# Grouping the diagonal blocks for the stream transposes, and writing out TensorE's order from the latents to the recurrence, in a two-layer RWKV-7/MLA decoder kernel

## The chip, the cores and the metric

The kernel runs on one core of a Trainium2 chip. TensorE multiplies matrices and writes PSUM; VectorE, ScalarE and GpSimd (POOL in the rows) work on SBUF and, but for GpSimd, on PSUM; SyncE (SP) issues nearly all DMAs. Every engine works through its own queue in order and waits on semaphores for the others. The metric is the device time of one execution in microseconds, the median of several runs. All data is float32.

## The reference

Two layers, each a mixer and a gated feed-forward, at 512 tokens and width 1024. The mixer projects once, runs an RWKV-7 time mix of 8 heads x 64 and a latent attention of 8 heads, and adds both under gates. What matters here is the state of the time mix and what is around it:

```
p = n @ w_in                                  # r, k, v, loras, MLA latents, gates
def step(state, inp):                         # 512 tokens, 8 heads, state 64x64
    sa = einsum('bhij,bhj->bhi', state, a_t)
    state = state * w_t + sa[..., None] * b_t + v_t[..., None] * k_t
    y_t = einsum('bhij,bhj->bhi', state, r_t)
y_a = group_norm(y) + bonus, gated, @ w_out_rwkv
q = rmsnorm(q_lat) @ w_q_up; kv = rmsnorm(kv_lat) @ w_kv_up; causal softmax attention
merged = sigmoid(g_A) * y_a + sigmoid(g_B) * y_b
h = h + merged @ w_out; h = h + conv_ffn(rmsnorm(h))
```

The kernel doesn't run the 512 steps one by one: it cuts them into 8 chunks of 64 tokens. Within a chunk the terms between tokens form a lower triangular 64x64 matrix for each head and chunk, and its inverse is needed; from chunk to chunk a state of 64x64 for each head is carried.

## The kernel before

Activations lie transposed, features on partitions and the 512 tokens along the free axis. All weights come as one stream of 512 KB units; `produce` loads one (SP), `parts` splits it in a rounded part on ScalarE (`whi`, L201) and a rest on VectorE (`wlo`, L202), and `Blocks` hands out 128x128 blocks. A product of a block is three matmuls (`mm3`, L246 to L248), a tile of 8 blocks (`wtile`) is 24 matmuls into one PSUM tile `acc`.

`mixer` runs in three pools. In `ta` (up to L596) the inputs of the time mix are made; at its end VectorE writes the masked chunk matrices `AM` (L569). In `ti` (L614 to L738) the following is done; names and lines are those of the profile:

- four latent tiles `lat` (L623 to L626, evicted by VectorE), their squares on ScalarE (L629), one addition of two squares on GpSimd (L630), column sums on TensorE (`tok_sums`, L305), a reciprocal root (`rsqrt_tok`: VectorE L285, GpSimd L286, ScalarE `nw` L288) and a spread by TensorE transposes (L294).
- L643: for each pair of chunks the products of AM and v, copied into `Z` by ScalarE (L647).
- the inverse of the triangular matrices. Each 64x64 matrix has two diagonal blocks of 32x32, so AM holds four groups of partitions ("quad") with 32 matrices each. VectorE transposes the four groups, one instruction each (L665), into `X`, then does a forward substitution of 30 steps on all of X at once (L669, L671), and transposes back: four times into AM (L674) and twice into `T11` (L676). The lower left block follows with TensorE: AM x T11 (L685), copied to `Q` by VectorE and ScalarE (L688), Q x the second diagonal block (L692), copied to AM (L696). This comes in two halves of 16 matrices (`b`).
- the recurrence over the 8 chunks c: state x AR (L709), `xs` on VectorE (L712), AM x xs (L718), copy to Z (L720), BT x Z (L726), and the new state `St` on VectorE (L733) from a product on GpSimd (L732). Each of the steps waits for the one before it.
- four gate tiles (`gate`), each a `wtile`, an eviction on VectorE (L436), a tanh on ScalarE (L450) and a store to `gate_d`.

In `tb` (from L740) come the value product `Vt` (L826), chunk outputs (L756, L764), group norm, and four attention head pairs (`heads`), with the projections, scores (L852), softmax, transposes (L863) and `po` (L870).

The order in each engine's queue isn't that of the source: Tile's scheduler sets it, so gate tiles and the attention of the first head pairs come to stand between the pieces of the inverse and of the recurrence, where it saw room. Weights keep their order in the stream: latents, the gate tiles, the up-projections.

Of the kernel before, what the change touches and what calls it, by code (L numbers as in the profile page):

```python
# [9 lines left out]
F32 = mybir.dt.float32  # L10
F32R = mybir.dt.float32r
I32 = mybir.dt.int32
AF = mybir.ActivationFunctionType
# [145 lines left out]
def build(ctx, tc, x, pos, wst, vecd, constd, out):  # L159
# [95 lines left out]

    def acc():
        return accp[-1].tile([128, 512], F32, name="acc", tag="acc")
# [23 lines left out]
    def rsqrt_tok(ps, n, eps, js=range(4), pool=sm, tag="nsq"):  # L281
# [5 lines left out]
        w = pool.tile([128, 512], F32, name="nw", tag=tag, bufs=1)  # L287
# [15 lines left out]
    def tok_sums(ps, sq, js=range(4)):  # L303
        for j in js:
            PE.matmul(ps[:, j:j + 1], sq[:, 128 * j:128 * j + 128], ones[:, 0:1], start=True, stop=True)  # L305
# [93 lines left out]
    def mixer(l, ops, nrm, wks):  # L399
        with ExitStack() as mx:  # L400
# [213 lines left out]
            with pool(name=f"ti{l}", bufs=2) as ti:  # L614
# [6 lines left out]
                lat = []  # L621
                for i in range(4):
                    ps = wtile(ops)  # L623
# [3 lines left out]
                sq = [ti.tile([128, 512], F32, name="lsq", bufs=3) for _ in range(3)]  # L627
                for i in range(3):
                    A.activation(sq[i], lat[i], AF.Square)  # L629
                G.tensor_tensor(sq[0], sq[0], sq[1], ALU.add)  # L630
                ws = []
                for i, (t, n) in enumerate(((sq[0], 256.0), (sq[2], 128.0))):
                    ssq = sc()
                    tok_sums(ssq, t)
                    ws.append(rsqrt_tok(ssq, n, NORM_EPS, pool=ti, tag=f"nw{i}"))


                for i in range(4):
# [10 lines left out]
                rq = tl.tile([128, 512], F32, name="rq", bufs=1)  # L649
                spread(ws[0], tabs[1], rq, sc)  # L650
                rk = ti.tile([128, 512], F32, name="rk", bufs=1)
                spread(ws[1], None, rk, sc)
                V.scalar_tensor_tensor(lat[2], lat[2], vc(l, "kv_norm"), rk, ALU.mult, ALU.mult)
                kp = tl.tile([128, 512], F32, name="kp", bufs=1)
                k2 = ti.tile([128, 512], F32, name="k2", bufs=1)
# [5 lines left out]
                X = ti.tile([128, 32, 32], F32, name="X", bufs=1)  # L661
                T11 = ti.tile([128, 32, 32], F32, name="T11", bufs=1)
                quad = [((0 if e else 64) + 32 * hf, (128 if e else 64) + 32 * hf, hf) for e in range(2) for hf in range(2)]
                for r0, c0, hf in quad:
                    V.transpose(X[r0:r0 + 32], AMu[r0:r0 + 32, :, c0:c0 + 32].rearrange("p u t -> p t u"))  # L665
                for s in range(1, 31):
                    tm = ti.tile([128, 256], F32, name="tm", tag="tm", bufs=2)
                    tm = tm[:, 0:(31 - s) * s].rearrange("p (a b) -> p a b", b=s)
                    V.tensor_tensor(tm, X[:, s + 1:32, s:s + 1].to_broadcast([128, 31 - s, s]),  # L669
                                    X[:, s:s + 1, 0:s].to_broadcast([128, 31 - s, s]), ALU.mult)  # L670
                    V.tensor_tensor(X[:, s + 1:32, 0:s], X[:, s + 1:32, 0:s], tm, ALU.add)  # L671
                V.memset(X.rearrange("p a b -> p (a b)")[:, 0:1024:33], 1.0)
                for r0, c0, hf in quad:
                    V.transpose(AMu[r0:r0 + 32, :, c0:c0 + 32].rearrange("p u t -> p t u"), X[r0:r0 + 32])  # L674
                    if hf == 0:
                        V.transpose(T11[r0:r0 + 32].rearrange("p u s -> p s u"), X[r0:r0 + 32].rearrange("p t s -> p s t"))  # L676
                gate(GATES[4][0], ti)
                half = [(64, 64), (0, 128)]
                for b in range(2):
                    us = range(16 * b, 16 * b + 16)  # L680
                    Q = ti.tile([128, 512], F32, name="Q", bufs=2).rearrange("p (u s) -> p u s", s=32)
                    ps = xyt()[:, b, :]
                    for u in us:
                        for r0, c0 in half:
                            PE.matmul(ps[r0 + 32:r0 + 64, 32 * (u % 16):32 * (u % 16) + 32], AMu[r0:r0 + 32, u, c0 + 32:c0 + 64],  # L685
                                      T11[r0:r0 + 32, u, :], start=True, stop=True, tile_position=(r0, r0 + 32))
                    for r0, c0 in half:
                        (A.copy if r0 else V.tensor_copy)(Q[r0 + 32:r0 + 64], ps[r0 + 32:r0 + 64, :].rearrange("p (u s) -> p u s", s=32))  # L688
                    ps = xyt()[:, b, :]
                    for u in us:  # L690
# [46 lines left out]
                for i in GATES[4][1:]:  # L737
                    gate(i, ti)  # L738
# [252 lines left out]
```

## Time and profile before

| what | value |
|---|---|
| median of 3 runs | 1616.56 us (1616.34 to 1618.22) |
| profiled execution | 1616.36 us |
| its span in the trace | 1614.6 us |
| TensorE busy | 97% of the span |
| VectorE, ScalarE, GpSimd busy | 58%, 40%, 12% |

Stages of the first layer in that trace: the last AM is there at 184.9 us, the latents begin at 183.0, the first matmul of the inverse at 234.7, the recurrence runs from 256.4 to 301.3. The second layer goes through the same some 796 us later. A busy matmul row is a modelled one, so "busy" says that the engine didn't wait, not that it ran at its peak; the granted clock is read beside it.

### The profile page before, as it was taken

Reading aid. Unit: us, or ns where it says so; the run is one execution under the profiler, and the core shown is the slowest. Engines: PE = TensorE matmul, PEld = TensorE weight load, DVE = VectorE, ACT = ScalarE, POOL = GpSimd, SP = SyncE. Lnnn points to the kernel's source line nnn. Section 1 sums busy time; section 2 is a strip of 40 time slices with the busy share of each in tenths; the row PEclk is TensorE's granted clock in tenths of the full one; section 3 lists DMA queues with packets and bytes.
Section 4 is the critical chain, followed back from the end, with each engine's and each line's share of the span. In section 5 each row is a group of like instructions: output and inputs, shape, how many; then the busy total and the mean of one; then the engine's idle time right before and its main releaser. Section 6 shows DMA issues by size and latency. Waiting matters only on the chain.

```text
span 1614.6 us, 22337 instructions
## 1 busy us (share of the span) xinstructions
PE 1568.8 (97%) x9014; PEld 1259.1 (78%) x9014; DVE 942.0 (58%) x1482; ACT 651.0 (40%) x987; POOL 190.4 (12%) x158
## 2 busy tenths in 40 slices
PE   8999989999999999999999999899999999999997
PEld 6888766668888888888877887666788888888886
DVE  6578786666545555533347668857564555554333
ACT  6446334563434333422245342346533433333221
POOL 1011101300211101100011111023003111110000
PEclk9999999999999999999999999899999999999998
DMA  6333312224322323233343233212243223232232
GB/s 212 107 111 119 114 57 86 67 73 156 124 90 94 104 92 102 94 108 121 111 150 98 98 98 111 73 47 82 92 156 116 90 93 104 92 101 95 95 101 79
DMA packets 57848, 166.08 MB, mean 103 GB/s; under 512 B 6416, under 2 KB 9616, under 8 KB 57744
## 3 DMA queue, kind: packets, MB, share of 16 engines
q1 hardware_dynamic: 57600, 164.48, 31.1%
q8 instruction: 71, 1.16, 0.3%
q14 instruction: 33, 0.27, 0.1%
q10 hardware_dynamic: 144, 0.16, 0.0%
HBM read 147.32 MB, written 17.30 MB: 102 GB/s over the span
## 4 chain that ended last, share of the span: by engine, by line
PE 79%; issue 10%; DVE 7%; POOL 2%; ACT 1%; DMA 0%; POOLq 0%; DVEq 0%; SPq 0%; ACTq 0%
PE acc L246 22%; PE acc L248 22%; PE acc L247 22%; PE sc L852 2%; PE po L870 2%; PE xy L718 1%; PE pt L863 1%; DVE AM L674 1%; DVE X L665 1%; DVE wlo L202 1%; POOL mu L781 1%; PE m L566 1%; DVE tm L669 1%; DVE X L671 1%; POOL nv L286 1%
## 5 line engine op out<-in xcount | busy, mean ns | idle before, releaser
L246 PE MATMUL acc<-hi,whi 128*128 128x512 f32 (+1 forms) x1910 | 751.4, 393 | 8.4 <-ACT hi L267 5.3
L248 PE MATMUL acc<-hi,wlo 128*128 128x512 f32 (+1 forms) x1910 | 747.1, 391 | 0.7 <-DVE wlo L202 0.7
L247 PE MATMUL acc<-lo,whi 128*128 128x512 f32 (+1 forms) x1910 | 745.7, 390 | 0.0
L201 ACT CAST whi<-raw 128x1024 fp32r<-128x1024 f32 (+2 forms) x249 | 253.3, 1019 | 541.0 <-PE acc L247 479.3
L246 PEld LDWEIGHTS acc<-hi,whi 128*128 128x128 f32 x1910 | 360.9, 189 | 83.6 <-ACT hi L267 5.3
L248 PEld LDWEIGHTS acc<-hi,wlo 128*128 128x128 f32 x1910 | 361.2, 189 | 77.4 <-issue 2.1
L247 PEld LDWEIGHTS acc<-lo,whi 128*128 128x128 f32 x1910 | 361.2, 189 | 73.4 <-issue 1.2
L202 DVE TENSOR_TENSOR wlo<-raw,whi 128x1024 fp32r<-128x1024 f32 (+2 forms) x249 | 308.3, 1239 | 182.0 <-ACT whi L201 181.2
L942 POOL TENSOR_TENSOR c<-c,rstd 128x512 f32<-128x512 f32 x44 | 57.3, 1304 | 377.9 <-ACT c L941 377.9
L935 DVE TENSOR_TENSOR u<-acc,rstd 128x512 f32<-128x512 f32 x44 | 30.3, 691 | 100.2 <-PE acc L248 94.4
L944 DVE TENSOR_TENSOR c<-c,acc 128x512 f32<-128x512 f32 x44 | 30.2, 687 | 82.4 <-POOL c L942 82.4
L941 ACT ACTIVATE c<-c 128x512 f32<-128x512 f32 x44 | 27.6, 632 | 78.7 <-DVE c L940 78.7
L286 POOL TENSOR_TENSOR nv<-nv,cst 128x4 f32<-128x4 f32 (+1 forms) x10 | 12.8, 1288 | 332.8 <-DVE nv L285 332.8
L321 POOL TENSOR_TENSOR nacc<-nacc,nsq 128x512 f32<-128x512 f32 x14 | 25.0, 1788 | 201.7 <-ACT nsq L320 201.7
L858 ACT ACTIVATE P<-P,mn 128x128 f32<-128x128 f32 (+3 forms) x64 | 35.5, 556 | 26.1 <-DVE mn L855 22.8
L852 PE MATMUL sc<-K,q 128*128 128x128 f32 (+3 forms) x128 | 44.5, 447 | 0.0
L424 DVE TENSOR_TENSOR cur<-acc,rstd 128x512 f32<-128x512 f32 x28 | 19.1, 690 | 43.0 <-PE acc L248 38.5
L436 DVE TENSOR_TENSOR gg<-acc,rstd 128x512 f32<-128x512 f32 x28 | 19.2, 686 | 36.9 <-PE acc L248 36.7
L860 ACT ACTIVATE P<-P,mn 128x128 f32<-128x128 f32 (+3 forms) x64 | 34.8, 558 | 8.8 <-DVE mn L859 8.8
L870 PE MATMUL po<-PT,Vt 128*64 128x128 f32 x320 | 37.5, 286 | 0.8 <-DVE PT L865 0.8
L938 ACT ACTIVATE c<-u,vec 128x512 f32<-128x512 f32 x44 | 35.4, 809 | 2.3 <-DVE u L935 1.5
L855 DVE CUSTOM_DVE_ANT_0 P<-sc,cst 128x128 f32<-128x128 f32 (+3 forms) x64 | 30.6, 480 | 9.2 <-PE sc L852 5.3
(233 smaller groups left out, 1393.8 us busy)
## 6 DMA issues: line engine op xcount, KB each, us to landing
raw<-in_w SPq DMA_DIRECT2D x238, 512.0 KB, 3.4
gate_d<-gg SPq DMA_DIRECT2D x32, 256.0 KB, 2.1
AM<-gate_d SPq DMA_DIRECT2D x16, 256.0 KB, 4.6
gb<-gate_d SPq DMA_DIRECT2D x16, 256.0 KB, 3.7
h<-in_x SPq DMA_DIRECT2D x8, 256.0 KB, 4.3
rgate_d<-gt SPq DMA_DIRECT2D x8, 256.0 KB, 3.0
bl_d<-rk SPq DMA_DIRECT2D x8, 256.0 KB, 2.0
bl<-bl_d SPq DMA_DIRECT2D x8, 256.0 KB, 2.6
```

What stands on the lines that cost most here:

```text
L201: A.copy(hi, r)
L202: V.tensor_tensor(lo, r, hi.bitcast(F32), ALU.subtract)
L246: PE.matmul(ps, w[0], xx[0], start=first, stop=False)
L247: PE.matmul(ps, w[0], xx[1], start=False, stop=False)
L248: PE.matmul(ps, w[1], xx[0], start=False, stop=last)
L852: PE.matmul(sp[:, 0:n], qs[hh][:, 128 * b:128 * b + 128], ks[hh][:, 0:n], start=True, stop=True)
L855: V.tensor_tensor_reduce(out=P[:, 0:n], in0=sp[:, 0:n], in1=cst[:, C_CAUS + 512 - n:C_CAUS + 512], scale=-ATT_SCALE, scalar=1e30, op0=ALU. ...
L858: A.activation(P[:, 0:n], P[:, 0:n], AF.Exp, bias=mn[:, 0:1], scale=-1.0, accum_out=mn[:, 1:2])
L860: A.activation(P[:, 0:n], P[:, 0:n], AF.Copy, scale=mn[:, 2:3])
L870: PE.matmul(po[64 * hh:64 * hh + 64, 128 * b:128 * b + 128], Vt[:, kb, 64 * hd:64 * hd + 64], PTs[hh][:, 128 * kb:128 * kb + 128], start=k ...
L938: A.activation(cc, u[:, 2:514], AF.Identity, bias=vc(l, "conv_b", i), scale=vc(l, "conv_w", 2 * FT + i))
L942: G.tensor_tensor(cc, cc, rstd, ALU.mult)
```

## The change

The stretch in `ti` is written anew.

- The four diagonal groups are first copied side by side into a tile `DX` (two copies on VectorE, two on ScalarE), and one transpose of all 128 partitions makes X. After the substitution one transpose makes `T11`, one makes `T22`, and ScalarE copies T22 back into AM in four copies. L735 (before: L692) reads its block from T22, not from AM.
- This code stands ahead of the latents in the source, where it was behind them.
- TensorE's instructions in `ti` keep the order of the source (`tc.manual_schedule`); the other engines' orders are still the scheduler's. For this a class `Part` computes a tile in pieces: latents and gate tiles are cut into groups of `mm3` and put between the other steps by hand.
- The inverse's TensorE part comes in one piece of 32 matrices instead of two of 16.
- In the recurrence a `filler()` stands behind L760 and behind L770 (before: L709, L718), one `mm3` each, as long as the last two gate tiles have any.
- The sum of the first two squares is made by TensorE (`tok_sums` takes a list), not by GpSimd.

```
+            with pool(name=f"ti{l}", bufs=2) as ti, tc.manual_schedule(engines={PE.engine}):
+                for r0, c0, hf in quad:
+                    (A.copy if hf else V.tensor_copy)(DX[r0:r0 + 32], AMu[r0:r0 + 32, :, c0:c0 + 32])
+                V.transpose(X, DX.rearrange("p u t -> p t u"))
...
+                V.transpose(T11.rearrange("p u s -> p s u"), X.rearrange("p t s -> p s t"))
+                T22 = ti.tile([128, 32, 32], F32, name="T22", tag="dx", bufs=1)
+                V.transpose(T22.rearrange("p u t -> p t u"), X)
+                for r0, c0, hf in quad:
+                    A.copy(AMu[r0:r0 + 32, :, c0:c0 + 32], T22[r0:r0 + 32])
...
+                parts4 = [Part(ops, lat_end) for _ in range(4)] + [gpart(i) for i in GATES[4]]
+                for i in range(3):
+                    parts4[i].go()
+                a_ak_v(0)
+                w0 = lsum(0, sq[0:2], 256.0)
+                parts4[3].go(4)
+                w1 = lsum(1, sq[2], 128.0)
+                parts4[3].go()
...
+                spread(w0, tabs[1], rq, sc)
+                a_ak_v(1)
...
+                spread(w1, None, rk, sc)
...
+                parts4[4].go(4)
+                a_ak_v(2)
+                parts4[4].go()
+                a_ak_v(3)
+                parts4[5].go()
...
-                for r0, c0, hf in quad:
-                    V.transpose(X[r0:r0 + 32], AMu[r0:r0 + 32, :, c0:c0 + 32].rearrange("p u t -> p t u"))
...
-                for r0, c0, hf in quad:
-                    V.transpose(AMu[r0:r0 + 32, :, c0:c0 + 32].rearrange("p u t -> p t u"), X[r0:r0 + 32])
-                    if hf == 0:
-                        V.transpose(T11[r0:r0 + 32].rearrange("p u s -> p s u"), X[r0:r0 + 32].rearrange("p t s -> p s t"))
-                gate(GATES[4][0], ti)
...
+                parts4[6].go(2)
...
+                rest = iter([(parts4[6], 1)] * 4 + [(parts4[7], 1)] * 8)
+                def filler():
+                    for part, n in (next(rest, (None, 0)),):
+                        if part:
+                            part.go(n)
...
+                        filler()
                         xs = tl.tile([128, 4, 2, 64], F32, name="xs", bufs=1)
...
+                    filler()
                     V.tensor_copy(Z[ur:ur + 64, i, e, :].rearrange("p (q h i) -> p q h i", h=2, i=64),
...
-                for i in GATES[4][1:]:
-                    gate(i, ti)
```

TensorE's queue around the inverse's lower left block, first layer, before (L685 is AM x T11, L692 is Q x the second diagonal block, L246 to L248 are gate tiles):

```order
869 L248 MATMUL acc<-hi,wlo 128x512
870 L685 MATMUL xy<-T_1912,AM 32x32 x31
871 L246 MATMUL acc<-hi,whi 128x512
872 L247 MATMUL acc<-lo,whi 128x512
873 L692 MATMUL xy<-AM,Q 32x32 x32
874 L248 MATMUL acc<-hi,wlo 128x512
```

The same place now (L724 is AM x T11, L735 is Q x T22):

```order
846 L248 MATMUL acc<-hi,wlo 128x512
847 L724 MATMUL xy<-T_1656,AM 32x32 x64
848 L246 MATMUL acc<-hi,whi 128x512
849 L247 MATMUL acc<-lo,whi 128x512
850 L248 MATMUL acc<-hi,wlo 128x512
851 L246 MATMUL acc<-hi,whi 128x512
852 L247 MATMUL acc<-lo,whi 128x512
853 L248 MATMUL acc<-hi,wlo 128x512
854 L735 MATMUL xy<-T_1754,Q 32x32 x64
```

Both halves of the 32 matrices go in one, and two groups of a gate tile stand between L724 and L735.

ScalarE's queue around the copies of Q, first layer, before (L201 splits a weight unit, L450 is a gate's tanh, L267 splits a latent, L688 is Q, L696 the copy into AM):

```order
144 L201 CAST whi<-raw 128x1024 x2
145 L688 COPY Q<-xy 32x512
146 L450 ACTIVATE gg<-gg 128x512
147 L267 ACTIVATE hi<-lat_1687,vec 128x512
148 L696 COPY AM<-xy 32x16x32
```

The same place now (L651 copies T22 into AM, L467 is the tanh, L729 is Q, L739 the copy into AM):

```order
146 L201 CAST whi<-raw 128x1024
147 L651 COPY AM<-T_1754 32x32x32 x4
148 L467 ACTIVATE gg<-gg 128x512
149 L729 COPY Q<-xy 32x512 x2
150 L739 COPY AM<-xy 32x16x32 x2
```

The four copies of T22 stand ahead of Q in ScalarE's queue.

TensorE's queue in one step of the recurrence, between BT x Z (L726) and the next step's state x AR (L709), before (L852 are attention scores, L246 a projection):

```order
944 L852 MATMUL sc<-K,q 128x128
945 L726 MATMUL xy<-Z,BT_205 64x64 x2
946 L726 MATMUL xy<-Z,BT_206 64x64 x2
947 L726 MATMUL xy<-Z,BT_207 64x64 x2
948 L726 MATMUL xy<-Z,BT_208 64x64 x2
949 L246 MATMUL acc<-hi,lk_2550 128x512
950 L852 MATMUL sc<-K,q 128x128
951 L852 MATMUL sc<-K,q 128x256
952 L709 MATMUL xy<-St,AR_201 64x64 x2
```

A step of the recurrence now (L770 is AM x xs, L779 is BT x Z, L760 is state x AR):

```order
876 L770 MATMUL xy<-xs,AM 64x64 x8
877 L246 MATMUL acc<-hi,whi 128x512
878 L247 MATMUL acc<-lo,whi 128x512
879 L248 MATMUL acc<-hi,wlo 128x512
880 L779 MATMUL xy<-Z,BT_205 64x64 x2
881 L779 MATMUL xy<-Z,BT_206 64x64 x2
882 L779 MATMUL xy<-Z,BT_207 64x64 x2
883 L779 MATMUL xy<-Z,BT_208 64x64 x2
884 L760 MATMUL xy<-St,AR_201 64x64 x2
```

One group of a gate tile stands behind L770, none between L779 and L760; the attention's matmuls have moved behind the recurrence.

## Rows read from the trace of the kernel before

**Rows 1.** The page's first part: busy time, share and instructions of TensorE and others.

```profile
PE 1568.8 (97%) x9014; PEld 1259.1 (78%) x9014; DVE 942.0 (58%) x1482; ACT 651.0 (40%) x987; POOL 190.4 (12%) x158
```

**Rows 2.** Stretches: length, busy time of each engine, TensorE's mean granted clock, DMA share.

```profile
206.00:260.00 54.00, 44.66 (x539) 34.91 (x538) 43.30 (x71) 19.80 (x30) 2.31 (x2) 0.87 0.21 69
260.00:300.00 40.00, 39.62 (x428) 28.14 (x428) 23.52 (x59) 17.50 (x40) 8.62 (x13) 1.00 0.12 41
300.00:340.00 40.00, 37.70 (x424) 25.50 (x423) 29.21 (x87) 28.44 (x68) 13.15 (x11) 1.00 0.32 100
1000.00:1060.00 60.00, 50.03 (x607) 39.02 (x605) 46.96 (x79) 21.53 (x32) 4.64 (x6) 0.91 0.24 80
257.00:262.00 5.00, 3.89 (x55) 2.77 (x53) 3.03 (x4) 1.75 (x3) 1.76 (x4) 1.00 0.40 136
```

**Rows 3.** Waits of TensorE from 206 to 260: us in total, times, longest.

```profile
PE xy L685 <- DVE T L676: 3.6, 2, 1.9
PE sc L294 <- ACT nw L288: 3.3, 2, 3.2
PE acc L246 <- DVE gg L436: 1.5, 1, 1.5
```

**Rows 4.** Timeline of TensorE in the recurrence: start, length, line, tiles, count, wait.

```profile
258.42 0.69 PE L726 MATMUL xy<-Z,BT 128*64 128x64 f32 x16
260.09 0.68 PE L709 MATMUL xy<-St,AR 64*64 64x64 f32 x16 [0.99 <-DVE St L735]
...
261.56 1.14 PE L718 MATMUL xy<-xs,AM 64*64 64x64 f32 x16
```

**Rows 5.** Timeline of VectorE, the first transpose ahead of the substitution and behind it.

```profile
184.95 2.03 DVE L665 STREAM_TRANSPOSE X<-AM 32x1024 f32<-32x1024 f32 x1
...
230.73 2.06 DVE L674 STREAM_TRANSPOSE AM<-X 32x1024 f32<-32x1024 f32 x1
```

**Rows 6.** Timeline of VectorE in the recurrence.

```profile
258.35 1.23 DVE L202 TENSOR_TENSOR wlo<-raw,whi 128x1024 fp32r<-128x1024 f32 x1
259.61 0.42 DVE L735 COPY St<-xy 128x256 f32<-128x256 f32 x1
260.82 0.68 DVE L712 TENSOR_TENSOR xs<-xy,Z 64x512 f32<-64x512 f32 x1 [0.78 <-PE xy L709]
262.73 0.68 DVE L720 COPY Z<-xy 64x512 f32<-64x512 f32 x1 [1.23 <-PE xy L718]
```

**Rows 7.** Waits of VectorE from 193.08 to 230.73, from first latent to last substitution.

```profile
DVE gg L436 <- PE acc L248: 2.0, 1, 2.0
DVE lat L653 <- ACT rk L298: 0.9, 1, 0.9
DVE rq L300 <- PE sc L294: 0.3, 1, 0.3
```

**Rows 8.** Timeline of TensorE from the latents to the first matmul of the inverse.

```profile
194.96 0.50 PE L248 MATMUL acc<-hi,wlo 128*128 128x512 f32 x1 [0.35 <-DVE wlo L202]
...
205.56 1.84 PE L305 MATMUL sc<-cst,lsq 128*128 128x1 f32 x16
...
230.83 0.39 PE L246 MATMUL acc<-hi,whi 128*128 128x512 f32 x1
...
234.69 0.22 PE L685 MATMUL xy<-T,AM 32*32 32x32 f32 x2 [1.65 <-DVE T L676]
```

**Rows 9.** Timeline of TensorE, second half of the inverse's last product.

```profile
253.74 1.20 PE L692 MATMUL xy<-AM,Q 32*32 32x32 f32 x64
254.87 0.50 PE L246 MATMUL acc<-hi,whi 128*128 128x512 f32 x1
```

**Rows 10.** Timeline of ScalarE: a weight cast, a gate's tanh, a copy of Q.

```profile
188.55 1.05 ACT L201 CAST whi<-raw 128x1024 fp32r<-128x1024 f32 x1 [4.68 <-PE acc L247]
...
243.05 0.63 ACT L450 ACTIVATE gg<-gg 128x512 f32<-128x512 f32 x1 [0.82 <-DVE gg L436]
...
251.59 0.58 ACT L688 COPY Q<-xy 32x512 f32<-32x512 f32 x1 [2.36 <-PE xy L685]
```

More of the change, by code (lines that the diff above doesn't have):

```diff
@@ L254, in wtile, with __init__, go @@
         return ps
+    class Part:
+        def __init__(self, ops, end):
+            self.ops, self.end, self.i, self.ps = ops, end, 0, None
+        def go(self, n=8):
+            if self.i == 0:
+                self.ps = acc()
+            for _ in range(min(n, len(self.ops) - self.i)):
+                mm3(self.ps, W.get(), self.ops[self.i], self.i == 0, self.i == len(self.ops) - 1)
+                self.i += 1
+                if self.i == len(self.ops):
+                    self.end(self.ps)
     def acc():
@@ L303, in tok_sums @@
     def tok_sums(ps, sq, js=range(4)):
+        sq = sq if isinstance(sq, list) else [sq]
         for j in js:
-            PE.matmul(ps[:, j:j + 1], sq[:, 128 * j:128 * j + 128], ones[:, 0:1], start=True, stop=True)
+            for i, t in enumerate(sq):
+                PE.matmul(ps[:, j:j + 1], t[:, 128 * j:128 * j + 128], ones[:, 0:1], start=i == 0, stop=i == len(sq) - 1)
     class Norm:
@@ L626, in mixer, with a_ak_v @@
                     lat.append(o)
[L627 to L638, printed above, removed]
+                    if i < 3:
+                        sq.append(ti.tile([128, 512], F32, name="lsq", tag="lsq", bufs=3))
+                        A.activation(sq[i], o, AF.Square)
+                def a_ak_v(i):
                     ps = xyt()
@@ L666, in mixer @@
[L666 to L672, printed above, removed]
@@ new lines, in mixer @@
+                half = [(64, 64), (0, 128)]
+                Q = ti.tile([128, 32, 32], F32, name="Q", bufs=1)
+                ps = xyt()
+                for u in range(32):
+                    for r0, c0 in half:
+                        PE.matmul(ps[r0 + 32:r0 + 64, u // 16, 32 * (u % 16):32 * (u % 16) + 32],
+                                  AMu[r0:r0 + 32, u, c0 + 32:c0 + 64], T11[r0:r0 + 32, u, :],
+                                  start=True, stop=True, tile_position=(r0, r0 + 32))
+                for b in range(2):
+                    for r0, c0 in half:
+                        (A.copy if r0 else V.tensor_copy)(Q[r0 + 32:r0 + 64, 16 * b:16 * b + 16, :],
+                                                          ps[r0 + 32:r0 + 64, b, :].rearrange("p (u s) -> p u s", s=32))
@@ L695, in mixer @@
+                parts4[6].go(2)
+                ps = xyt()
+                for u in range(32):
+                    for r0, c0 in half:
+                        PE.matmul(ps[r0:r0 + 32, u // 16, 32 * (u % 16):32 * (u % 16) + 32], Q[r0 + 32:r0 + 64, u, :],
+                                  T22[r0 + 32:r0 + 64, u, :], start=True, stop=True, tile_position=(r0 + 32, r0))
+                for b in range(2):
                     for r0, c0 in half:
                         (A.copy if r0 else V.tensor_copy)(AMu[r0:r0 + 32, 16 * b:16 * b + 16, c0 + 32:c0 + 64],
-                                                          ps[r0:r0 + 32, :].rearrange("p (u s) -> p u s", s=32))
+                                                          ps[r0:r0 + 32, b, :].rearrange("p (u s) -> p u s", s=32))
```

60 lines of the change are left out of this document (31 added, 29 removed).

## The prediction

> **What bounds the kernel now.** I read the page's first part, then the clock and busy times by stretch, then TensorE's waits and its timeline through the stretch that the change touches, then the queues of VectorE and ScalarE there. TensorE is busy for 1568.8 of 1614.6 us [rows 1]: only its waits, its slow stretches and its own work can move the end. The change touches one stretch of each layer. There the first layer loses 54 - 44.66 = 9.3 us between 206 and 260 and the second 60 - 50.03 = 10.0 us between 1000 and 1060, and the mean granted clock is 0.87 and 0.91 [rows 2]. The clock has two levels, so half speed lasted 54 x 0.13 x 2 = 14.0 us and 60 x 0.09 x 2 = 10.8 us. Work at half speed takes twice its time: about half of these 24.8 us, 12 us, is lost. Stretch and clock together cost some 31 us over both layers; that is what can be won. Three waits make the first layer's loss: 3.3 us for the norms' column (nw), 3.6 us for the transposed block T11, 1.5 us for a gate tile's eviction [rows 3]; about 1 us is a state wait [rows 4].
>
> **The transposes.** Before, ten transposes of 32 rows stand on VectorE: four ahead of the substitution, six behind it, 2.03 us and 2.06 us in the rows shown [rows 5], some 20 us. Now there are two copies of 32x1024 on VectorE (two more on ScalarE at the same time) and three transposes of 128 rows. No row shows one on 128 rows. It costs between 2.0 us, if all rows go at once, and 8.1 us, if it works as four; I take 2.0, since every 32-row one here handles 1024 elements in a row and takes 2 us. The Trainium skill's page "VectorE: DVE Perf Modes", section "The three transpose paths", says that one instruction gives a 4x4 grid of independently transposed 32x32 blocks; by that the price is the lower end, and no run here shows it yet. A copy of 1024 elements I put at 1.05 us, between 0.68 for half as many [rows 6] and 1.23 for a subtraction [rows 6]. So X stands at 184.95 + 2.1 + 2.0 = 189.1. From lat0's eviction to the last step VectorE took 193.08 to 230.73, 37.65 us, of which it waited 2.0 + 0.9 + 0.3 = 3.2 [rows 7]; the new order holds the same instructions there, 34.5 us, and in a walk through it I find no wait of size, so T11 begins at 223.6 and is there at 225.5, T22 at 227.5. Before, the first of them began at 230.73 and the last ended at 242.3.
>
> **TensorE's arrival.** Before, it reached the first T11 matmul at 234.69 - 1.65 = 233.0 [rows 8]. Nine matmuls of the third gate tile, which start at 230.83 [rows 8], no longer stand ahead: 230.8. Away go also the waits for nw (3.3) and for wlo (0.35, [rows 8]) and what the first half-speed stretch cost, half of 7.0 less the 0.4 waited in it, 3.3; four more column sums come in, half of the 1.8 us that eight take [rows 8]: 0.9. That is 224.7. The nw wait is gone because VectorE, 4 us less behind, hands over the sums' reciprocal root earlier, and all eight matmul groups of lat3 now lie between the sums and the first spread. So TensorE waits about 0.8 us for T11 instead of 3.6.
>
> **The new wait.** L724 and L735 are now 64 matmuls each, twice the 1.13 us of 32 [rows 9], 2.3 us. L724 runs to 227.85 and six gate matmuls to 229.35 (nine took 2.2). L735 needs Q, half of which ScalarE copies. In ScalarE's new order Q stands behind four copies of T22 into AM, and those wait for T22 at 227.5. Each has 1024 elements: 1.05 us, as the cast [rows 10] (512 take 0.58 [rows 10]). 227.5 + 4.2, the gate's tanh 0.63 [rows 10], two Q copies 1.16: 233.4. TensorE stands still for 4.0 us, with only two gate groups as cover, which end long before. Behind it the AM copies cost 0.1.
>
> **The recurrence.** Before, its three waits a step were covered by attention work; now a group of three gate matmuls stands in two of the three places. Rows: L709 ends at 260.77, xs runs 260.82 to 261.50, L718 starts at 261.56 [rows 4, 6]: 0.79 us, which a group of 0.75 to 0.8 fills. L718 ends at 262.70 and Z takes 0.68 [rows 4, 6]: filled likewise. Between L726 and the next L709 nothing stands any more: L726 ends at 259.1, L709 starts at 260.09, 0.99 us idle, of which VectorE's wlo, ending 259.58, made 0.4 [rows 4, 6]. So 0.55 a step without such a delay, and 0.1 for the other two places: 7 x 0.65 = 4.6. wlo stands ahead of St in two steps (0.4 each) and three latent subtractions in one (0.5), while one value matmul group fills one place (-0.6). Taken: 5.0 us a layer, against 1.1 before. The idle after it, 0.4 and 2.3 us up to 340 [rows 2], I leave as it is: attention loses the recurrence as cover, but chunk outputs and the next heads' projections stand there, and I allow 3 us a layer either way.
>
> **The sum.** Idle after: 0.8 + 4.0 + 0.1 + 5.0 = 9.9 a layer, 19.8 in both, against 19.3: +0.5. Clock: a standstill of 3.2 us came ahead of one drop and the T11 and gate waits ahead of the other [rows 3]; the 4.0 us will bring one drop a layer. Taken as 7 us long and 3 lost (some of it falls on waits): 6 against 12, -6.0. Column sums +1.8. Interruptions of gate tiles: the first matmul behind one shows 0.50 instead of 0.39 [rows 8, 9]; seven fewer a layer at 0.1 to 0.2: -2.4. The wlo waits, 0.35 a layer: -0.7. POOL's addition of two squares goes and was hidden; gate tanh and store move with their tiles on ScalarE and SP, where nothing waits for them. Sum -6.8. The profiled execution took 1616.4 us (span 1614.6), 0.2 below the median, so 1609.6 there and **1609.8 us** as median.
>
> **The rivals.** *Nothing gained* (1614.5): the first softmaxes stand behind group norm's reductions in VectorE's queue, with no recurrence left to cover them, and each layer gives back 2 to 3 us. For it: ScalarE was busy 28.4 of 40 us in that phase [rows 2]. Against it: TensorE lost only 2.3 there. *Slower, by the clock* (1622): for 34 us a layer TensorE now runs small matmuls with a gap every 4.6 us. Should the clock fall twice more a layer, 3.4 us each, that is 13.6 us, and 1609.8 becomes some 1623; from one more drop a layer on, the gain is gone. Against it: from 257 to 262, with 1.1 of 5 us idle and the same pieces, the clock stayed at 1.00 [rows 2]. The Trainium skill's page "TensorE: Matmul & The Clock Gate", section "A second HAM failure mode: psum-queue depth-cycling", says that short idles between matmul groups can be frequent enough to make the clock oscillate; by that this rival holds, and the stretch just named does not agree. *The grouping does not serve four*: 128 rows cost 8.1 us. X comes 6 us later and T11, T22 6 each: 18 us a layer, 1645. *The stall is covered* (1599): shorter ScalarE copies and no drop, 4 to 5 us a layer more.
>
> **How the numbers follow.** Forecast 0.62, nothing gained 0.17, clock 0.10, transposes 0.05, covered 0.06. The range runs from the covered case's upper half to the beginning of the clock case: 1600 to 1618. About 0.2%, 3.2 us, is what a measurement can tell. Faster than 1613.3: most of the forecast (0.57) and the covered case, 0.63. Within: the rest and most of the nothing-gained case, 0.21. Slower: 0.16.
>
> **What would show it.** Right: three transposes near 2 us; no nw wait; a T11 wait under 1.5; about 4 us before L735 that ends with ScalarE's Q; seven St gaps of 0.5 to 1; one half-speed stretch a layer. Wrong: transposes near 8 us, half speed within the recurrence, or attention gaps above 6 us a layer.

## The result, and the profile after

The changed kernel takes **1623.9 us** (median) beside 1616.0 for the kernel before: ratio 1.0038, interval 1.0028 to 1.0049. It is slower: by 7.9 us between the medians, by 6 us by the ratio, in which the few short executions count too. The forecast was 1609.8 us, and its range, 1600 to 1618, does not hold the time. Most executions of this kernel lie at 1621.6 to 1626.1 us, a few at 1611.6 to 1612.6, none between. The profiled one, of the first kind, took 1624.1 us (span 1622.3, 7.7 more than before).

The page's first part, which answers to [rows 1], and the stretches that answer to [rows 2] (length; busy time of PE, PEld, DVE, ACT, POOL; mean granted clock; DMA share and GB/s):

```profile
PE 1578.6 (97%) x9030; PEld 1265.6 (78%) x9030; DVE 915.6 (56%) x1472; ACT 661.3 (41%) x999; POOL 184.6 (11%) x156
```
```profile
206.00:260.00 54.00, 46.86 (x564) 36.93 (x563) 29.44 (x56) 17.33 (x25) 2.33 (x3) 0.75 0.14 50
260.00:300.00 40.00, 37.03 (x502) 27.30 (x503) 20.20 (x34) 10.88 (x17) 7.86 (x10) 0.82 0.31 95
1000.00:1060.00 60.00, 52.50 (x666) 42.66 (x666) 40.93 (x84) 22.74 (x31) 3.48 (x4) 0.91 0.18 60
257.00:262.00 5.00, 4.40 (x37) 3.35 (x36) 3.01 (x5) 1.89 (x3) 0.01 (x1) 0.50 0.24 67
```

VectorE has 26 us less to do, and TensorE waits less from 206 to 260 (54 - 46.86 = 7.1 us against 9.3). What is worse is the clock: 0.75 against 0.87 from 206 to 260, 0.82 against 1.00 from 260 to 300. From 257 to 262, where the row of before had 1.00, it is 0.50. TensorE's waits from 206 to 345 (us in total, times, longest), which answer to [rows 3]:

```profile
PE xy L735 <- DVE Q L729: 5.6, 1, 5.6
PE xy L760 <- DVE St L786: 3.4, 5, 1.0
PE sc L903 <- DVE q L895: 1.0, 1, 1.0
PE xy L760 <- DVE St L788: 0.5, 1, 0.5
PE xy L724 <- DVE T L647: 0.4, 1, 0.4
```

The nw and gate waits are gone, and T11's is 0.4 us instead of 3.6. In their place stands one wait of 5.6 us at L735, ahead of the recurrence. Where the clock fell and rose, by stretches of the same view (the last two are the second layer):

```profile
229.20:234.80 5.60, 0.03 (x3) 0.04 (x3) 1.37 (x2) 3.90 (x6) 0.00 (x0) 0.84 0.39 140
...
233.06:270.60 37.54, 34.09 (x334) 25.62 (x334) 12.83 (x20) 5.46 (x8) 2.89 (x4) 0.50 0.09 27
...
270.60:285.30 14.70, 12.56 (x163) 9.20 (x162) 7.33 (x11) 2.72 (x4) 3.51 (x6) 1.00 0.05 19
...
287.67:291.08 3.41, 3.41 (x25) 2.34 (x23) 0.86 (x2) 1.90 (x3) 0.00 (x0) 0.50 0.41 154
...
1038.60:1048.84 10.24, 7.48 (x145) 6.60 (x146) 2.73 (x4) 1.94 (x4) 0.00 (x0) 0.50 0.08 29
...
1049.00:1090.00 41.00, 36.48 (x508) 26.84 (x507) 21.93 (x34) 10.89 (x17) 6.40 (x10) 1.00 0.19 64
```

In the first layer the clock falls within the 5.6 us standstill (mean 0.84) and stays at half until 270.6, through the first four steps of the recurrence. Then it is full, but for 3.4 us from 287.7 on, in the recurrence's last step, behind a St wait of 0.99 us. In the second layer the same instructions follow much the same standstill (5.8 us), and the clock is back at 1048.8. TensorE's timeline in the recurrence, with steps at half speed, the end of the long fall, and steps at full speed (it answers to [rows 4]):

```profile
254.14 1.12 PE L760 MATMUL xy<-St,AR 64*64 64x64 f32 x16 [0.60 <-DVE St L786]
...
261.96 1.12 PE L760 MATMUL xy<-St,AR 64*64 64x64 f32 x16 [0.60 <-DVE St L786]
...
269.12 0.80 PE L877 MATMUL acc<-whi,hi 128*128 128x512 f32 x1
...
270.68 0.68 PE L760 MATMUL xy<-St,AR 64*64 64x64 f32 x16
...
275.44 0.68 PE L760 MATMUL xy<-St,AR 64*64 64x64 f32 x16 [0.60 <-DVE St L786]
...
280.20 0.68 PE L760 MATMUL xy<-St,AR 64*64 64x64 f32 x16 [0.60 <-DVE St L786]
```

A step takes 261.96 - 254.14 = 7.82 us at half speed and 4.76 at full; the St wait is 0.60 in both. The clock came back as a triple of L877 (the value product; a triple is one group of three 128x512 matmuls) stood for the first time where the other steps wait for St. To add it up, the whole of what the change touches, in both layers, first before and then after:

```profile
180.00:345.00 165.00, 152.64 (x1551) 113.08 (x1550) 123.32 (x263) 76.19 (x154) 25.87 (x27) 0.96 0.23 74
985.00:1150.00 165.00, 151.40 (x1541) 110.09 (x1540) 121.89 (x277) 80.36 (x169) 25.87 (x27) 0.97 0.22 68
```
```profile
180.00:345.00 165.00, 153.70 (x1495) 113.64 (x1493) 102.92 (x238) 74.06 (x145) 23.04 (x26) 0.88 0.22 71
985.00:1150.00 165.00, 152.56 (x1568) 113.17 (x1566) 110.49 (x261) 82.22 (x164) 23.04 (x26) 0.97 0.25 79
```

Idle falls from 26.0 to 23.7 us. Half speed rises from 165 x (0.04 + 0.03) x 2 = 23 us to 165 x (0.12 + 0.03) x 2 = 50 us. Some of it falls on waits, so here is TensorE's busy time in the stretches at half speed, summed, first before (213.0 to 219.8, 243.7 to 250.6, 1011.7 to 1015.1, 1039.0 to 1045.9), then after (the three stretches at 0.50 above):

```profile
sum 23.89, PE 23.50 PEld 18.14 DVE 20.15 ACT 11.44 POOL 0.81; mean PE 5.87 PEld 4.54 DVE 5.04 ACT 2.86 POOL 0.20
```
```profile
sum 51.19, PE 44.98 PEld 34.57 DVE 16.42 ACT 9.30 POOL 2.89; mean PE 14.99 PEld 11.52 DVE 5.47 ACT 3.10 POOL 0.96
```

Half of the work between, (44.98 - 23.50) / 2 = 10.7 us, is lost. 10.7 - 2.3 = 8.4; measured are 7.7. So waits did not cost the time. The clock did, nearly all of it in one layer.

### The profile page after: what moved, and what is told of

The parts are those of the page before. It is cut to its first block, busy times and chain, and to the rows that moved or that the text cites. A ratio compares the mean times of both kernels' runs of the same rounds, so it can differ in the third digit from the quotient of the medians.

```text
span 1622.3 us, 22442 instructions
## 1 busy us (share of the span) xinstructions
PE 1578.6 (97%) x9030; PEld 1265.6 (78%) x9030; DVE 915.6 (56%) x1472; ACT 661.3 (41%) x999; POOL 184.6 (11%) x156
## 4 chain that ended last, share of the span: by engine, by line
PE 82%; issue 10%; DVE 5%; ACT 2%; POOL 1%; DMA 0%; SPq 0%; POOLq 0%; DVEq 0%; ACTq 0%
PE acc L246 23%; PE acc L247 22%; PE acc L248 22%; PE sc L903 2%; PE po L921 2%; PE pt L914 1%; PE xy L770 1%; PE m L583 1%; PE xy L760 1%; DVE wlo L202 1%; PE m L591 1%; ACT AM L651 1%; PE xy L779 1%; PE m L567 0%; POOL nv L301 0%
## 5 line engine op out<-in xcount | busy, mean ns | idle before, releaser
L246 PE MATMUL acc<-hi,whi 128*128 128x512 f32 (+1 forms) x1910 | 754.8, 395 | 5.3 <-ACT hi L282 5.2
L248 PE MATMUL acc<-hi,wlo 128*128 128x512 f32 (+1 forms) x1910 | 745.3, 390 | 0.0
L201 ACT CAST whi<-raw 128x1024 fp32r<-128x1024 f32 (+2 forms) x249 | 253.3, 1019 | 587.1 <-PE acc L247 514.0
L246 PEld LDWEIGHTS acc<-hi,whi 128*128 128x128 f32 x1910 | 360.7, 189 | 80.7 <-ACT hi L282 5.2
L248 PEld LDWEIGHTS acc<-hi,wlo 128*128 128x128 f32 x1910 | 361.0, 189 | 74.3
L921 PEld LDWEIGHTS po<-PT,Vt 128*64 128x64 f32 x320 | 22.0, 136 | 21.6 <-issue 7.3
```

The costliest lines, as they stand in the source:

```text
L201: A.copy(hi, r)
L246: PE.matmul(ps, w[0], xx[0], start=first, stop=False)
L248: PE.matmul(ps, w[1], xx[0], start=False, stop=last)
L921: PE.matmul(po[64 * hh:64 * hh + 64, 128 * b:128 * b + 128], Vt[:, kb, 64 * hd:64 * hd + 64], PTs[hh][:, 128 * kb:128 * kb + 128], start=k ...
```

## The experiments

**Theory 1**: the standstill before L735 lowers the clock, and the recurrence behind it, where short waits alternate with small matmuls and one triple of gate matmuls a place, does not bring it back. **Rival A**: the recurrence's mix lowers the clock by itself. **Rival C** (named after the first runs): the 128 matmuls of 32x32 at L724 and L735 lower it. All edits are against the changed kernel, unless it says otherwise. The table takes idle and half speed from the profiled execution of each, both layers, worked out as above from the stretches of 165 us. The ratio is to the kernel before as it ran along with each.

| kernel | median us (lowest to highest) | ratio to before, interval | idle | half speed |
|---|---|---|---|---|
| before | 1616.0 | 1 | 26.0 | 23 |
| changed | 1623.9 (1611.6 to 1626.1) | 1.0038, 1.0028 to 1.0049 | 23.7 | 50 |
| e1_t22_pool | 1610.0 (1604.0 to 1626.0) | 0.9979, 0.9950 to 1.0008 | 18.0 | 43 |
| e2_gates_front | 1615.1 (1613.0 to 1618.8) | 1.0001, 0.9992 to 1.0010 | 24.5 | 20 |
| e3_group_only | 1605.5 (1603.9 to 1607.4) | 0.9941, 0.9929 to 0.9953 | 18.1 | 13 |
| e4_order_only | 1647.5 (1626.1 to 1650.3) | 1.0172, 1.0131 to 1.0213 | 31.3 | 96 |
| e5_q_covered | 1612.1 (1609.2 to 1614.8) | 0.9978, 0.9969 to 0.9986 | 19.5 | 30 |
| e6_covered_pool | 1603.7 (1602.4 to 1607.4) | 0.9930, 0.9918 to 0.9942 | 16.1 | 10 |
| e7_sched_rec | 1590.8 (1589.4 to 1591.9) | 0.9846, 0.9834 to 0.9859 | 8.2 | 7 |
| e8_copy_by_bank | 1620.3 (1608.2 to 1631.1) | 1.0032, 1.0012 to 1.0053 | 20.4 | 43 |
| e9_sched_rec_alone | 1600.9 (1598.9 to 1605.7) | 0.9915, 0.9900 to 0.9930 | 15.4 | 20 |
| e10_pairs | 1616.0 (1611.7 to 1619.3) | 1.0002, 0.9992 to 1.0013 | 23.8 | 30 |
| e11_bare_rec | 1604.0 (1603.3 to 1604.4) | 0.9930, 0.9918 to 0.9942 | 18.3 | 20 |

One profile is one execution, but the mean granted clock of all of them is on record. It was 0.984 or less in 17 of the 20 executions of the changed kernel and in 11 of the 12 of e8_copy_by_bank, and 0.986 or less in 6 of the 12 of e1_t22_pool. In the 61 executions of e2, e3, e5, e6, e7, e9, e10 and e11 it was never under 0.987 (before: 0.989 to 0.993). So the long fall came in most executions of the kernels that have the changed kernel's recurrence behind a wait of 2 us or more (e4_order_only too, 0.966 to 0.987); where the triples stood otherwise, the means point to none.

### Which half of the change costs

The grouping alone, in the kernel before, with TensorE's order left to the scheduler:

```diff
-                    V.transpose(X[r0:r0 + 32], AMu[r0:r0 + 32, :, c0:c0 + 32].rearrange("p u t -> p t u"))
+                    (A.copy if hf else V.tensor_copy)(DX[r0:r0 + 32], AMu[r0:r0 + 32, :, c0:c0 + 32])
+                V.transpose(X, DX.rearrange("p u t -> p t u"))
...
+                V.transpose(T11.rearrange("p u s -> p s u"), X.rearrange("p t s -> p s t"))
+                T22 = ti.tile([128, 32, 32], F32, name="T22", tag="dx", bufs=1)
+                V.transpose(T22.rearrange("p u t -> p t u"), X)
...
+                    A.copy(AMu[r0:r0 + 32, :, c0:c0 + 32], T22[r0:r0 + 32])
...
```

> The kernel before with the grouping alone: DX, one 128-partition transpose in, T11 and T22 out, four copies of T22 into AMu on ScalarE; TensorE's order left to the scheduler as before (k2 and rk share the squares' buffers, so that DX has room). T11 is ready some 12 us before it was in the kernel before. Theory 1: the two waits on T11 (1.65 and 1.90 us) go, the nw and gg waits (3.17 and 1.54) stay and with them the drops of 6.8 us each; 1611 to 1615. If the grouping itself caused the loss (its copies on ScalarE in front of Q): 1618 or more, with a standstill of 3 us or more at Q.

It gained more than that: 1605.5. Its waits of TensorE from 200 to 300:

```profile
PE sc L294 <- ACT nw L288: 2.1, 2, 1.8
PE xy L688 <- DVE T L675: 1.1, 1, 1.1
```

The T11 wait fell from 3.6 to 1.1 as expected; that the nw wait would fall too, from 3.3 to 2.1, because VectorE reaches the norms' sums sooner (L285 at 208.3 us, before 211.3), was missed, and so was the clock: half speed went to 13 us in both layers. Idle is 7.9 us less than before, half speed 10 us less (5 lost): 12.9 us, and the span is 12.6 shorter. The grouping does all that it should. Its four copies on ScalarE do no harm here; the scheduler set ScalarE's first copy of Q ahead of them (229.5 and 230.1 us in the first layer), so this run doesn't try them in front of all of Q.

The order alone, with the old ten transposes:

```diff
-                    (A.copy if hf else V.tensor_copy)(DX[r0:r0 + 32], AMu[r0:r0 + 32, :, c0:c0 + 32])
-                V.transpose(X, DX.rearrange("p u t -> p t u"))
+                    V.transpose(X[r0:r0 + 32], AMu[r0:r0 + 32, :, c0:c0 + 32].rearrange("p u t -> p t u"))
...
-                    A.copy(AMu[r0:r0 + 32, :, c0:c0 + 32], T22[r0:r0 + 32])
+                    V.transpose(AMu[r0:r0 + 32, :, c0:c0 + 32].rearrange("p u t -> p t u"), X[r0:r0 + 32])
...
```

> The changed order on TensorE, gate tiles split, with the old ten transposes of one block each (no DX, no T22, no copies). T11 is complete only about 10 us after the 30 steps end, so TensorE should stand 8 to 12 us before L724 in each layer in place of 0.45, and hardly before L735. Theory 1: the clock drops in this standstill too and comes back slowly in the recurrence; 1624 to 1634. If the loss came from the copies of T22 and their wait alone, and not from a standstill as such: half speed under 20 us in all, 1614 to 1620.

1647.5, beyond the expected 1634. The standstill is there, as 9.3 us in two waits at L721 (AM x T11 here), and behind it the recurrence ran at half speed in both layers (waits; then stretches of the first and second layer):

```profile
PE xy L721 <- DVE T L648: 9.3, 2, 5.2
```
```profile
249.00:276.50 27.50, 25.78 (x199) 18.89 (x199) 10.06 (x17) 3.74 (x5) 2.88 (x4) 0.50 0.09 29
1041.00:1089.00 48.00, 40.61 (x470) 31.14 (x472) 21.75 (x26) 6.67 (x10) 2.89 (x4) 0.50 0.10 34
```

No copies of T22 exist here, and the same happens, worse. So the loss belongs to the order: waits ahead of this recurrence, whatever makes them. It doesn't take a long one: in the first layer the clock was back at 242.3 from the fall in the standstill, and fell again at 249.1, in the recurrence's first step, behind a wait of 1.2 us for AM. That fall lasted 27.3 us.

### The standstill stays, what follows it changes

Six of the recurrence's triples go into a row ahead of it:

```diff
-                parts4[6].go(2)
+                parts4[6].go()
+                parts4[7].go(2)
...
-                rest = iter([(parts4[6], 1)] * 4 + [(parts4[7], 1)] * 8)
+                rest = iter([(parts4[7], 1)] * 6)
```

> The standstill stays (about 5.6 us before L735); six of the twelve triples of gate tiles that lay one by one in the recurrence stand in a row before it, behind the AM copies (eight triples there in place of two), and the recurrence keeps six. Theory 1 (standstill lowers the clock, light work keeps it low): the longer dense row raises the clock before the recurrence begins; half speed in layer 0 falls from 37.6 us to 14 to 20, and the steps run at 4.8 to 5 us; the bare later steps cost 2 to 4 us a layer of idle; 1612 to 1618. Rival A (the recurrence's mix lowers the clock): half speed comes back within the recurrence, more of it since fewer triples stand there; 1624 to 1632.

1615.1, as theory 1 said. The standstill is the same (5.57 us), the clock falls in it, and is back in the row of triples after 10.2 us, in both layers; the recurrence then keeps it to its end:

```profile
233.30:243.60 10.30, 8.74 (x140) 7.64 (x141) 2.12 (x4) 1.73 (x3) 0.00 (x0) 0.50 0.04 15
243.60:300.00 56.40, 52.60 (x706) 37.77 (x707) 33.27 (x74) 23.15 (x48) 14.14 (x16) 1.00 0.26 85
```

All twelve in that row (parts4[6].go() and parts4[7].go() ahead, an empty rest):

> All twelve triples stand in front of the recurrence, behind the AM copies; none is left inside, other than what the scheduler sets there of attention's. The standstill before L735 stays at about 5.6 us. Theory 1: the clock drops once a layer for about 10 us and is back before the recurrence, which then holds full speed although it has no gate triples; 1609 to 1617. Rival A (the recurrence's light mix lowers the clock by itself): a second stretch at half speed within each recurrence, 7 us or more, 1617 to 1630.

1604.0, better than either said, with the same standstill of 5.58 us. The clock behaves as in the run before (10.2 and 6.8 us at half speed); after the drop the recurrence ran at full speed in both layers:

```profile
243.70:300.00 56.30, 55.49 (x572) 40.41 (x571) 32.58 (x78) 27.19 (x60) 8.63 (x13) 1.00 0.17 57
...
1032.20:1095.00 62.80, 61.98 (x712) 45.01 (x711) 37.65 (x93) 31.87 (x70) 10.06 (x15) 1.00 0.19 62
```

Idle from 243.7 to 300 is 0.8 us: with no gate triple left in its places, attention's matmuls fill them. This I had not expected; in the changed kernel the gate triples stand in these places and attention's come behind. So this recurrence is not bare, and the run doesn't test rival A as it was meant to.

The same twelve, in pairs at the first six places:

```diff
-                rest = iter([(parts4[6], 1)] * 4 + [(parts4[7], 1)] * 8)
+                rest = iter([(parts4[6], 2)] * 2 + [(parts4[7], 2)] * 4)
```

> The changed kernel with the recurrence's twelve triples in pairs at the first six places in place of one at each of twelve; nothing else moves. Theory 1: the first three steps have no St wait at half speed or a shorter one, and the clock comes back in the first or second step (half speed in layer 0 at 15 to 21 us in place of 37.6); 1613 to 1618. If the clock comes back only when some time has passed, or at attention's first triple (L877), whatever stands in the steps: half speed of 30 us or more, 1622 to 1626.

1616.0, in theory 1's range, and no execution as slow as the changed kernel's 1624. In the second layer the clock came back at 1042.7, right behind the first pair; in the first at 243.9, ahead of it, so that layer tells nothing of pairs. L877's first triple, in the expectation's words attention's, comes only at 259.6 and 1056.0, so the clock can come back without it. In the second layer it fell once more later, behind waits of 0.8 and 0.6 us:

```profile
1043.00:1063.00 20.00, 17.14 (x190) 12.60 (x184) 11.23 (x17) 6.35 (x9) 1.84 (x3) 1.00 0.18 62
1063.00:1070.00 7.00, 6.79 (x52) 5.06 (x53) 1.54 (x3) 1.56 (x3) 2.34 (x4) 0.51 0.35 126
```

So rival A is not empty: a gapped recurrence can lose the clock by itself, here for some 7 us, in the first layer of the changed kernel for 3.4. Beside the long fall these are small. The Trainium skill's page "TensorE: Matmul & The Clock Gate", section "A second HAM failure mode: psum-queue depth-cycling", says that frequent short idles between matmul groups make the clock oscillate; this last row agrees, while the row before it, with the same waits at full speed for 20 us, shows that they need not.

### What follows stays, the standstill shrinks

The copies of T22 go to GpSimd:

```diff
-                    A.copy(AMu[r0:r0 + 32, :, c0:c0 + 32], T22[r0:r0 + 32])
+                    G.tensor_copy(AMu[r0:r0 + 32, :, c0:c0 + 32], T22[r0:r0 + 32])
```

> The four copies of T22 into AMu (4.21 us on ScalarE, in front of the Q copies) go to GpSimd, which stands idle there; nothing else changes. PE's standstill before L735 (5.57 us in layer 0 and 5.82 in layer 1 of the changed kernel) should shrink to about 1.5 to 2.5 us. Theory 1 (the standstill lowers the clock, and the recurrence's mix behind it does not bring it back): with a short standstill there is no or one short stretch at half speed before the recurrence, half speed in both layers together falls from 51 us to 14 or less, and the time is 1624 less some 18 of clock and 7 of idle: 1597 to 1603. Rival A (the recurrence's own mix of 64-row matmuls and one triple per place lowers the clock, whatever stands ahead of it): half speed stays at 30 us or more, only the idle time goes: 1614 to 1618. Rival B (the copies on GpSimd come late and AM waits for them before L770): idle moves there, about 1622 to 1626.

The standstill fell to 2.3 and 2.6 us; GpSimd's four copies took 5.2 us, and nobody waited for them (rival B is out). But the times spread from 1604 to 1626, in three groups; the fastest is near theory 1's range, the others are not. The profiled execution (1617.8) shows both ends at once:

```profile
233.90:240.70 6.80, 6.80 (x132) 5.70 (x125) 1.36 (x2) 1.15 (x2) 0.52 (x1) 0.50 0.02 6
240.80:277.00 36.20, 31.70 (x394) 22.81 (x392) 19.05 (x29) 6.96 (x11) 6.40 (x10) 1.00 0.17 59
1025.80:1059.90 34.10, 31.73 (x268) 23.55 (x260) 11.88 (x18) 4.89 (x7) 2.71 (x4) 0.50 0.07 24
```

In one layer the clock was back by the recurrence's first St wait, and 36 us with 12% of waits ran at full speed. In the other it wasn't back, and the first four steps of the same recurrence ran at half. So the recurrence can go on at either level that it enters with, at half for some 29 us (from its first L770 at 1030.9); that is what theory 1 has to say, in place of "the standstill costs so much".

The end of the long fall is the same each time. There are five of them in the profiles: 37.6 us in the changed kernel, 34.1 here, 34.1 in e8_copy_by_bank, 27.3 and 47.8 in e4_order_only. All five end within 1.2 us of the end of the same triple (L877, in e4 L874), the first that stands where TensorE otherwise waits for St. By e10_pairs it isn't this triple as such. Whether the St waits keep the clock down or the share of small matmuls, no run tells apart: from 234.8 to 245.8 TensorE worked 11 us without such a wait in the changed kernel, and the clock stayed at half.

Eight triples between L724 and L735 in place of two, the copies left on ScalarE:

```diff
-                parts4[6].go(2)
+                parts4[6].go()
                 ps = xyt()
...
-                parts4[6].go(2)
+                parts4[7].go(2)
...
-                rest = iter([(parts4[6], 1)] * 4 + [(parts4[7], 1)] * 8)
+                rest = iter([(parts4[7], 1)] * 6)
```

> All waits stay as in the changed kernel; TensorE's order alone is changed: eight triples of gate tile 6 stand between L724 and L735 in place of two, two triples of the last gate tile behind L735, six left for the recurrence. By the changed kernel's trace Q is ready 6.9 us after L724 ended, and eight triples at full clock take about 5.3 us, so the standstill should shrink to about 1.6 us with the copies on ScalarE untouched. Theory 1 (the standstill, not the copies, lowers the clock): half speed at or under 14 us in both layers together; idle 3 to 4 us a layer less; 1600 to 1607. Rival C (the 128 matmuls of 32x32 at L724 and at L735 lower the clock themselves): a drop of 7 to 10 us in each layer as in the run with the gates in front, 1607 to 1612.

The standstill fell to 1.62 us as expected, and the clock dropped all the same, for 13.6 us in each layer (in which TensorE also waited 1.85 us for AM): 1612.1, rival C's number and not theory 1's, though its drop was to be 7 to 10 us. With the copies on GpSimd as well:

> The run before this one with the copies of T22 on GpSimd as well: Q is ready about 3.6 us after L724 ends, under the eight triples. Theory 1: no standstill before L735, about 1 us before the recurrence, and no drop, or one of 3.4 us; 1595 to 1601. Rival C: the drop at L724 and L735 stays, 7 us a layer; 1601 to 1606. If the recurrence with six triples cannot hold the clock: half speed inside it, over 1610.

1603.7, at rival C's price, but not by its mechanism. L735 follows the triples without a wait, and in the first layer there is no drop at all; in the second it begins at 1028.8, as a wait of 2.05 us for AM has ended, behind L735:

```profile
225.00:260.00 35.00, 29.75 (x505) 22.68 (x504) 20.85 (x26) 10.34 (x15) 7.19 (x8) 1.00 0.21 66
...
1028.80:1035.60 6.80, 6.80 (x54) 4.95 (x52) 1.85 (x4) 0.62 (x1) 0.61 (x1) 0.50 0.01 2
```

As the only cause rival C falls: L724 and L735 stand here in both layers, and the full speed of the first outlasts them. A wait of some 2 us beside them can be enough for a drop, though, and theory 1 had taken that as harmless. Whether these small matmuls help such a wait to lower the clock is not shown.

The Q and AM copies shared out by PSUM bank, not by partitions:

```diff
-                        (A.copy if r0 else V.tensor_copy)(Q[r0 + 32:r0 + 64, 16 * b:16 * b + 16, :],
+                        (A.copy if b else V.tensor_copy)(Q[r0 + 32:r0 + 64, 16 * b:16 * b + 16, :],
...
```

> The changed kernel with the four Q copies and the four AM copies shared out by PSUM bank (ScalarE one bank, VectorE the other) in place of by partitions (both engines in each bank), so that no copy waits for the other engine's. The standstill before L735 should fall from 5.57 to about 4.3 us, and the one before L770 should go: the four copies take about 1.3 us in place of 2.6. Theory 1: the standstill still lowers the clock; 1612 to 1621, spread over two levels as the changed kernel's runs were. If the time falls to 1607 or less, the copies' order was what kept the clock down.

The standstill fell to 4.0 us, by 1.6 (expected 1.3), and the time stayed at 1620.3: the first layer spent 34 us at half speed again. So the length of the wait at L735, between 4.0 and 5.6 us, is worth its own microseconds and no more, as long as the clock falls in it and the same recurrence follows. But the copies did not run side by side as the expectation had it. VectorE's pair of Q ended before ScalarE's began, and behind L735 ScalarE's pair waited for VectorE's:

```profile
237.42 1.38 DVE L739 COPY AM<-xy 32x512 f32<-32x512 f32 x2 [6.12 <-PE xy L735]
...
238.89 1.16 ACT L739 COPY AM<-xy 32x512 f32<-32x512 f32 x2 [4.57 <-DVE AM L739]
```

### The version to keep

e6_covered_pool, with TensorE's source order ended behind the AM copies; and the same one edit in the changed kernel alone:

```diff
-            with pool(name=f"ti{l}", bufs=2) as ti, tc.manual_schedule(engines={PE.engine}):
+            with pool(name=f"ti{l}", bufs=2) as ti:
+                ms = tc.manual_schedule(engines={PE.engine})
+                ms.__enter__()
...
+                ms.__exit__(None, None, None)
                 St = [None]
```

> The changed kernel with one edit: TensorE's source order ends behind the AM copies, so that the scheduler places the recurrence; the copies on ScalarE, the order up to there and the standstill of about 5.6 us before L735 stay. Theory 1 (the standstill lowers the clock, the recurrence's short waits with one triple per place keep it low): the drop stays, but attention's matmuls fill the steps and end it early: half speed 10 to 17 us a layer in place of 37.6 and 10.2; the St waits go, 3 to 5 us a layer; 1603 to 1612. If the length of the low clock is set by the standstill alone: 37 us in at least one layer, 1614 to 1620.

And for the whole version, whose "run before" is e6_covered_pool:

> The run before this one with TensorE's source order ended behind the AM copies: the recurrence is placed by the scheduler again, as in the kernel before, which sets attention's matmuls between its waits. The recurrence's St waits (0.5 to 1.0 us, five to seven a layer) should go; clock as in the run before. 1592 to 1600 by theory 1; if the scheduler's order of attention brings back its own waits (gate tiles late, PSUM buffers held), 1600 to 1608.

The edit alone gave 1600.9. Not for the reason expected: the standstill did not stay, since the triples behind the end of the source order are now free to move ahead, and ten triples stand between L724 and L735 in place of two (its wait is 1.03 us). In both layers TensorE also paused for 1.8 us within L735, for no reason that the profile shows, and the clock fell there for 6.8 us. So this run doesn't tell the two apart. Together with the rest it gave **1590.8 us**, ratio 0.9846, the fastest kernel here. Its stretches, both layers:

```profile
180.00:345.00 165.00, 160.88 (x1634) 118.82 (x1633) 116.70 (x282) 88.57 (x181) 28.54 (x30) 1.00 0.24 79
985.00:1150.00 165.00, 160.89 (x1582) 118.11 (x1582) 107.85 (x255) 83.50 (x175) 28.54 (x30) 0.98 0.24 78
```

Against before, 17.8 us of idle and 8 us of clock are gone: 26, and the span is 24.7 shorter.

## Why the prediction was wrong

- **The transposes: right.** VectorE's timeline, which answers to [rows 5]: the two copies, X, T11, T22.

```profile
185.25 1.38 DVE L638 COPY DX<-AM 32x1024 f32<-32x1024 f32 x2
187.39 2.10 DVE L639 STREAM_TRANSPOSE X<-DX 128x1024 f32<-128x1024 f32 x1 [0.75 <-ACT DX L638]
...
223.08 2.19 DVE L647 STREAM_TRANSPOSE T<-X 128x1024 f32<-128x1024 f32 x1
225.13 1.97 DVE L649 STREAM_TRANSPOSE T<-X 128x1024 f32<-128x1024 f32 x1
```

  Four groups of rows cost what one did: 2.10, 2.19 and 1.97 us. The Trainium skill's page "VectorE: DVE Perf Modes", section "The three transpose paths", says that this transpose gives a 4x4 grid of 32x32 blocks, each transposed by itself; these rows agree. A DX copy took 0.69 us on VectorE, not 1.05, but ScalarE's pair took 2.1, and X waited for it. T11 stood at 225.3 (said: 225.5).
- **TensorE's arrival: right.** 225.0 (said: 224.7), no nw wait, and a T11 wait of 0.45 (said: 0.8).
- **The new wait: the place was right, the size wrong**, 5.57 instead of 4.0 us. ScalarE and VectorE, behind T22:

```profile
227.13 4.21 ACT L651 COPY AM<-T 32x1024 f32<-32x1024 f32 x4 [1.26 <-DVE T L649]
231.37 0.63 ACT L467 ACTIVATE gg<-gg 128x512 f32<-128x512 f32 x1
232.02 0.58 ACT L729 COPY Q<-xy 32x512 f32<-32x512 f32 x1
233.35 0.58 ACT L729 COPY Q<-xy 32x512 f32<-32x512 f32 x1 [0.75 <-DVE Q L729]
```
```profile
232.63 0.68 DVE L729 COPY Q<-xy 32x512 f32<-32x512 f32 x1 [3.89 <-ACT Q L729]
233.96 0.68 DVE L729 COPY Q<-xy 32x512 f32<-32x512 f32 x1 [0.64 <-ACT Q L729]
```

  The working put two Q copies of ScalarE behind the tanh, and took VectorE's as done by then. They alternate, each waiting for the other engine's, 2.6 us in place of 1.2. Shared out by bank, VectorE's pair is done while ScalarE still copies T22, and only ScalarE's own 1.17 us stand behind the tanh (e8_copy_by_bank). What puts the two engines in order is not shown: by e8's copies into AM it isn't only that both read one bank.
- **The recurrence's idle: right, a little high.** 3.9 us in the first layer, in six St waits (said: 5.0, in seven); attention's waits as small as taken.
- **The clock: this step failed.** "The 4.0 us will bring one drop a layer. Taken as 7 us long and 3 lost": the drop came, but lasted 37.6 us in the first layer (5.6 x 0.16 x 2 = 1.8 in the standstill, 35.8 behind it) and 10.2 in the second, and 3.4 more came in the first layer's recurrence: 51 us at half speed in place of 14. The clock was meant to give 6 us back and took 10.7. The length came from the drops of before (6.8 us at most), behind which TensorE worked without a pause (6.1 us behind the first, 5.8 behind the second). Here the recurrence follows, with its fillers spread thin.
- **The rival that held** is *Slower, by the clock*: its time, 1622 to 1623, is nearly the measured one, its mechanism only half. It expected two more short falls a layer; there was one long fall, in one layer, and one short one in the recurrence's last step. What spoke against it, the stretch from 257 to 262 of before at 1.00 with the same pieces, was read for the wrong question. That row shows that such work can keep full speed, which e1, e2 and the changed kernel's second layer confirm; whether it brings full speed back after a fall, it could not show.

So the cause that is shown is the fall of the clock together with the order behind it. Open: why the clock comes back in time in some executions of the changed kernel and in some layers, and not in others. The Trainium skill's page "TensorE: Matmul & The Clock Gate", section "Part 1: The HAM clock gate (the "warmup" mystery)", says that the number of slow matmuls varies between runs of one kernel; the two groups of times agree, and no run here shows what decides it.

## What to carry to other kernels

When a change moves a wait, look at what TensorE does behind it, not only at how long it is: here rows of 128x512 matmuls ended a drop of the clock within 10.2 us (e2, e11), and small ones with short waits between them could carry it on for 29 us and more. So put the dense filler into the wait or right behind it, ahead of the light part, and spread none of it thin. And an order written by hand should end where a scheduler has other work to fill with; here the grouping alone gave 10 us, the full hand order took more than that back, and the same order ended ahead of the recurrence gave 15, or 25 with eight triples between L724 and L735 and the copies on GpSimd as well.

## What the chip showed that was not expected

- The same recurrence ran its first four steps, some 29 us, at half speed in one layer and all its steps at full speed in the other, within one execution (e1_t22_pool): both levels last in it.
- A wait of 1.6 us next to the 32x32 matmuls was followed by a drop of 13.6 us in both layers (e5_q_covered), while a wait of 2.05 us, in the same execution, was followed by one in the second layer and by none in the first (e6_covered_pool).
- GpSimd copied 32x1024 elements in 1.0 to 1.9 us, ScalarE in 1.05, VectorE in 0.69.
